# A seven-product matrix multiplication: block sums of the weights formed by accumulating loads instead of VectorE

## The chip, the cores and the metric

One Trainium2 chip, one of its cores. The metric is the device time of one launch, in microseconds (us); lower is better. The engines are TensorE (PE in the profile; its weight loads are PEld), VectorE (DVE), ScalarE (ACT), GpSimd (POOL) and SyncE (SP). SyncE and GpSimd issue the transfers from and to DRAM (DMA); a transfer's issue is an instruction in the issuing engine's queue, and the transfer itself runs on 16 DMA engines.

## The reference

A trunk of two layers on a sequence of 512 tokens with width 1024, in float32. Layer 0 mixes tokens by chunked attention, layer 1 by a chunked spatial gate; each is followed by a squared-ReLU net. All are preceded by a norm that is scaled and shifted by a conditioning vector.

```python
def chunked_spatial_gating(h, w_in, v_gain, w_s, b_s, w_out):
    z = jax.nn.gelu(h @ w_in, approximate=False)
    u, v = jnp.split(z, 2, axis=-1)
    v = rms_norm(v, v_gain).reshape(B, nw, SG_WINDOW, SG_GROUPS, SG_HALF // SG_GROUPS)
    ...
    return (u * vm.reshape(B, S, SG_HALF)) @ w_out

def squared_relu_mlp(h, w1, w2):
    return jnp.square(jax.nn.relu(h @ w1)) @ w2
...
for i in range(DEPTH):                       # DEPTH = 2
    mod = cond @ ada_w[i] + ada_b[i]
    sh1, sc1, g1, sh2, sc2, g2 = ...
    h = rms_norm(x, norm_mix[i]) * (1.0 + sc1) + sh1
    x = x + g1 * (attention(h) if i == 0 else spatial_gating(h))
    h = rms_norm(x, norm_ffn[i]) * (1.0 + sc2) + sh2
    x = x + g2 * squared_relu_mlp(h, ffn_w1[i], ffn_w2[i])
```

The net's hidden width is 4096, the gate's is 2 x 3072.

## The kernel before

**Precision.** Each float32 matrix is split into a high part (a cast to the matmul type float32r, by ScalarE) and a low part (the rest, by VectorE): class `Split`, lines 483 and 484, or lines 388 and 389 for plain weights. A product of two such matrices takes three matmuls (`mm3`, line 94), all of which are recorded at line 92. The operands live in 49 slots of 4 KB per partition of on-chip memory (`SL`), handed out in turn, so a load waits until the slot's last reader is through.

**Seven products.** Some weights are multiplied in a 2 x 2 block form with seven block products instead of eight (the Winograd form of Strassen's scheme): `seven`, line 616. The left matrix A (512 tokens by 1024) has blocks of 256 x 512, the weight B (1024 by 1024) has blocks of 512 x 512. With the blocks counted from 0, the products and the PSUM sums (z, y, v, w; each one bank per row tile) are

- 0: A00 B00 on z, 1: A01 B10 on y; C00 takes both
- 2: (A10 + A11)(B01 - B00) on v; C11 takes it
- 3: (A10 + A11 - A00)(B11 - B01 + B00) on z, behind product 0; C01 takes the sum
- 4: (A01 - A10 - A11 + A00) B11 on v, behind product 2; C01 takes the sum
- 5: (A00 - A10)(B11 - B01) on z; C10 and C11 take the sum
- 6: A11 (B10 - B11 + B01 - B00) on w; C10 takes it

`load` brings the four blocks of B, two transfers of 512 KB each, on SyncE's queue (line 625); `right` forms the differences on VectorE (line 631, 128 x 1024 elements an instruction) and splits them; `left.prep` forms the sums of A's blocks (line 530) and splits them; `mult` runs 24 matmuls of 512 columns (two row tiles `u`, four k, three terms) and then calls `put` for each row tile. `put` of class `Sum` copies the PSUM bank into the result on its first use (line 519, ScalarE) and adds it after that (line 517, VectorE). `put` of class `Gate` does the same (lines 1433 and 1435) and on the second use applies Gelu and a sum of squares (lines 1436 and 1438), and stores the tile to DRAM by GpSimd's queue (line 1410).

**Where it is used.** Eight weights: in each of the two nets, the first three quarters of the down projection (six weights, class `Spent` for the left side), and in the gate two of the three pairs of column blocks of v (two weights, class `Kept` for the left side, whose blocks are kept and reused). The remaining parts are plain products.

**Order.** `Run` (line 687) walks through a list of steps; a step's load is called `ll` steps ahead of its preparation and its preparation `lp` steps ahead of its product. In the nets (`ll` = `lp` = 3) a step of the up projection, also of 24 matmuls, is put between two of the seven products; in the third weight of each net the last two products have none between them. In the gate (`ll` = `lp` = 2) the 14 products of both weights follow one another. A planner with a model of the times orders each engine's queue, outside the stretches that fix TensorE's order by hand. Beside all this runs a queue of background work (`bg`, line 264) that loads and adds up the conditioning weights on VectorE (line 194); it is placed behind the last split (`mark`).

**Around the gate.** The first pair of v's column blocks is plain (`gate_tile`, line 442) and its second block's products stand directly ahead of the seven-product steps. Behind them `u_block` (line 1528) loads v back from DRAM.

## Time and profile before

| | us |
|---|---|
| median of three runs | 1412.46 (1410.62 to 1413.95) |
| the profiled execution | 1407.58, span 1405.8 |
| TensorE busy | 1383.6 (98%) |
| VectorE busy | 1021.7 (73%) |
| ScalarE busy | 711.3 (51%) |
| GpSimd busy | 15.7 (1%) |
| DMA engines, SyncE's queue | 45.9% of the span, 214.01 MB |

The profile is one execution. A group is a set of instructions of one line, engine and shape: its count, its busy time with the mean of one in ns, and the idle time of its engine ahead of them with what ended it ("released" it). The windows view gives busy times of the engines in a stretch of the span, the number of instructions behind each, TensorE's granted clock and the share of time that the DMA engines were busy. Idle time of an engine that isn't the bottleneck costs nothing.

### The profile page before, as it was taken

What the parts mean: (1) busy time and instruction counts of PE and PEld (TensorE: products, weight loads), DVE (VectorE), ACT (ScalarE), POOL (GpSimd) and SP (SyncE); (2) the same over time, 40 slices, a digit from 0 to 9 for tenths busy, and PEclk for the clock granted to TensorE, in tenths of its full rate; (3) what the DMA queues carried; (4) which work ended last, traced back from release to release, by engine and by line L of the source; (5) the groups of instructions that cost most, each with busy time, mean ns of one, the idle gap of its engine ahead of it and who ended that gap; (6) DMA issues with size and microseconds to landing.
All of it is one profiled execution on the core that took longest, in us unless ns stands there. A gap on an engine that the chain in (4) does not pass through costs nothing.

```text
span 1405.8 us, 18946 instructions
## 1 busy us (share of the span) xinstructions
PE 1383.6 (98%) x7226; PEld 1185.3 (84%) x7226; DVE 1021.7 (73%) x1494; ACT 711.3 (51%) x1229; POOL 15.7 (1%) x46
## 2 busy tenths in 40 slices
PE   9999998999999999999999999999999999999998
PEld 7899987789888888888888888888889988888887
DVE  7888998666667878777895746665677367766882
ACT  6547667555464544646586443223445455453630
POOL 0000000000000000000000000000000000000000
PEclk9999999999999999999999999999999999999999
DMA  9666566573253361456346535435437225242141
GB/s 374 242 172 206 162 174 195 179 270 106 75 195 119 123 222 60 138 192 240 135 157 236 184 100 176 151 127 165 142 113 270 76 90 180 71 140 90 31 165 60
DMA packets 85628, 221.53 MB, mean 158 GB/s; under 512 B 7960, under 2 KB 9376, under 8 KB 85536
## 3 DMA queue, kind: packets, MB, share of 16 engines
q1 hardware_dynamic: 83808, 214.01, 45.9%
q0 software_dynamic: 1728, 6.29, 1.1%
q8 instruction: 57, 0.93, 0.3%
q14 instruction: 35, 0.29, 0.1%
HBM read 197.21 MB, written 14.68 MB: 151 GB/s over the span
## 4 chain that ended last, share of the span: by engine, by line
PE 88%; DMA 5%; DVE 4%; ACT 2%; issue 1%; SPq 0%; DVEq 0%; ACTq 0%
PE p L92 86%; DMA s<-in_a_w_in 2%; DMA s<-in_ada_w 1%; PE p L1564 1%; DMA s<-in_a_w_out 1%; PE p L1238 1%; ACT s L483 1%; DVE s L1200 1%; PE p L315 1%; DVE s L1243 0%; DMA s<-in_b_w_in 0%; DVE s L955 0%; DMA s<-in_ffn_w 0%; DVE s L1267 0%; DVE s L1154 0%
## 5 line engine op out<-in xcount | busy, mean ns | idle before, releaser
L92 PE MATMUL p<-s,s 128*128 128x512 f32 (+2 forms) x6568 | 1322.6, 361 | 7.0 <-DVE nm L1200 2.0
L92 PEld LDWEIGHTS p<-s,s 128*128 128x128 f32 x6568 | 1109.5, 189 | 191.5 <-DVE nm L1200 3.0
L484 DVE TENSOR_TENSOR s<-s,s 128x1024 fp32r<-128x1024 f32 x234 | 280.0, 1220 | 115.5 <-ACT s L483 55.4
L483 ACT CAST s<-s 128x1024 fp32r<-128x1024 f32 x234 | 241.1, 1051 | 163.0 <-PE p L92 112.6
L389 DVE TENSOR_TENSOR s<-s,s 128x1024 fp32r<-128x1024 f32 x80 | 96.8, 1222 | 63.5 <-ACT s L388 51.1
L388 ACT CAST s<-s 128x1024 fp32r<-128x1024 f32 x80 | 83.5, 1051 | 92.6 <-DMA s<-in_b_w_in 36.2
L631 DVE TENSOR_TENSOR s<-s,s 128x1024 f32<-128x1024 f32 x64 | 77.6, 1220 | 32.0 <-DMA s<-in_ffn_w 31.6
L739 ACT ACTIVATE r<-p 128x512 f32<-128x512 f32 x64 | 38.1, 595 | 116.2 <-PE p L92 116.2
L194 DVE SCALAR_TENSOR_TENSOR s<-s,cs,s 128x1024 f32<-128x1024 f32 x70 | 89.6, 1280 | 5.7 <-DMA s<-in_ada_w 5.0
L517 DVE TENSOR_TENSOR s<-p,s 128x512 f32<-128x512 f32 x104 | 70.4, 685 | 19.1 <-PE p L92 17.9
L745 ACT ACTIVATE s<-r 128x256 f32<-128x256 f32 (+1 forms) x112 | 44.9, 443 | 1.2
L424 DVE TENSOR_TENSOR tr<-p,s 128x512 f32<-128x512 f32 (+1 forms) x33 | 22.0, 671 | 30.9 <-PE p L92 30.5
L1205 ACT ACTIVATE s<-s,nm 128x128 f32<-128x128 f32 (+3 forms) x64 | 36.0, 564 | 7.2 <-DVE nm L1200 5.6
L1200 DVE CUSTOM_DVE_ANT_0 s<-p,s 128x128 f32<-128x128 f32 (+3 forms) x64 | 29.7, 486 | 8.1 <-issue 4.7
L1569 ACT CAST s<-p 128x256 fp32r<-128x256 f32 x48 | 17.7, 370 | 34.9 <-PE p L1564 27.0
L530 DVE TENSOR_TENSOR s<-s,s 128x1024 f32<-128x1024 f32 x28 | 33.6, 1220 | 1.0 <-PE p L92 0.9
L1238 PE MATMUL p<-ident,s 128*128 128x128 f32 x160 | 25.0, 278 | 8.0 <-DVE s L1267 6.9
L304 ACT ACTIVATE s<-s 128x512 f32<-128x512 f32 x24 | 15.3, 638 | 33.9 <-DVE s L425 33.9
L1243 DVE TENSOR_TENSOR s<-p,s 128x512 fp32r<-128x512 f32 (+3 forms) x64 | 29.1, 485 | 3.7 <-ACT s L1242 3.3
L1570 DVE TENSOR_TENSOR s<-p,s 128x256 fp32r<-128x256 f32 x48 | 20.1, 418 | 15.4 <-ACT s L1569 15.4
L1242 ACT CAST s<-p 128x512 fp32r<-128x512 f32 (+3 forms) x64 | 24.9, 429 | 11.8 <-PE p L1238 11.4
L1543 DVE SCALAR_TENSOR_TENSOR s<-s,vr,gain 128x512 f32<-128x512 f32 x24 | 17.7, 748 | 16.8 <-PE p L92 11.7
(142 smaller groups left out, 755.5 us busy)
## 6 DMA issues: line engine op xcount, KB each, us to landing
s<-in_ffn_w SPq DMA_DIRECT2D x128, 512.0 KB, 4.6
s<-in_ada_w SPq DMA_DIRECT2D x96, 512.0 KB, 5.0
s<-in_b_w_in SPq DMA_DIRECT2D x48, 512.0 KB, 4.8
s<-in_b_w_out SPq DMA_DIRECT2D x24, 512.0 KB, 4.4
s<-in_a_w_in SPq DMA_DIRECT2D x22, 512.0 KB, 6.7
s<-s SPq DMA_DIRECT2D x64, 128.0 KB, 2.4
vd<-s POOLq DMA_DIRECT2D x12, 512.0 KB, 3.8
s<-vd SPq DMA_DIRECT2D x12, 512.0 KB, 3.6
```

Source lines behind the costliest of these rows:

```text
L92: T.matmul(ps, lhsT, rhs, start=start, stop=stop, skip_group_check=more)
L194: V.scalar_tensor_tensor(acc, r, ck, acc, ALU.mult, ALU.add)
L388: A.copy(hi, raw)
L389: engs[len(ids) // 2 % len(engs)].tensor_tensor(lo, raw, f32(hi), ALU.subtract)
L483: A.copy(self.hi, raw)
L484: mark[0] = V.tensor_tensor(self.lo, raw, f32(self.hi), ALU.subtract)
L517: V.tensor_tensor(dst, ps, dst, ALU.add)
L631: V.tensor_tensor(x[0], y_[0], z[0], ALU.subtract)
L739: A.activation(r, ps, AF.Relu)
L745: A.activation(d, v, AF.Square)
L1200: V.tensor_tensor_reduce(out=pt[it], in0=ps[:, 0:n], in1=b["bias"][:, 512 - n:512], scale=-1.0, scalar=-NEG, op0=ALU.add, op1=ALU.min, acc ...
L1238: T.transpose(ps[:, it * P:(it + 1) * P], b["pt"][it][:, jt * P:(jt + 1) * P], ident)
```

## The change

The scheme is rewritten with the signs of some blocks turned, so that every right operand is a running sum of blocks of B. Three tiles are loaded: x = B00, z = B10, y = B11. After a tile's split has been read, an accumulating transfer adds the next block of B from DRAM into the same tile: x becomes B00 + B01, then + B11, then + B10; y becomes B11 + B01. These transfers are issued on GpSimd's queue (`G.dma_start` with `accum_op`). The minus signs go to the left sums and to `put`, which now takes the operation (add or subtract). The products run in the order 0, 1, 2, 4, 3, 5, 6 on the sums z, y, v, v, z, z, z: product 6 goes onto the open sum z, and C10 takes that sum alone. In the gate C10 is read by Gelu from PSUM (`whole`). The left sum for product 3 is formed together with that for product 4.

```diff
-        def put(self, t, hf, ps):
+        def put(self, t, hf, ps, op=ALU.add, whole=True):
 ...
-                V.tensor_tensor(dst, ps, dst, ALU.add)
+                V.tensor_tensor(dst, dst, ps, op)
...
@@ class Spent, prep (class Kept alike)
-                self.comb("x", (1, 0), (1, 1), ALU.add)
-            elif m == 3:
+                self.comb("x", (1, 0), (1, 1), ALU.subtract)
+            elif m == 4:
                 self.comb("x", "x", (0, 0), ALU.subtract)
-            elif m == 4:
-                self.comb((0, 1), (0, 1), "x", ALU.subtract)
+                self.comb((0, 1), (0, 1), "x", ALU.add)
...
@@ seven
-        def load(i, j):
-            raw[i, j] = []
+        def block(i, j, s_):
+            r0 = i * 512 + s_ * 256
+            return src[r0:r0 + 256, j * 512:j * 512 + 512].rearrange("(k p) n -> p k n", p=P)
+
+        def load(name, i, j):
+            raw[name] = []
             for s_ in range(2):
                 t, n = SL.get([P, 2, 512], F32)
-                r0 = i * 512 + s_ * 256
-                SP.dma_start(t, src[r0:r0 + 256, j * 512:j * 512 + 512].rearrange("(k p) n -> p k n", p=P))
-                raw[i, j].append((t, n))
-
-        def sub(d, a, b):
-
-            for x, y_, z in zip(raw[d], raw[a], raw[b]):
-                V.tensor_tensor(x[0], y_[0], z[0], ALU.subtract)
...
-        def right(m):
-            if m == 2:
-                sub((0, 0), (0, 1), (0, 0))
-            elif m == 3:
-                sub((0, 0), (1, 1), (0, 0))
-            elif m == 5:
-                sub((0, 1), (1, 1), (0, 1))
-            elif m == 6:
-                sub((1, 0), (1, 0), (0, 0))
...
+                SP.dma_start(t, block(i, j, s_))
+                raw[name].append((t, n))
+
+        def right(m, name, add):
+
+            op[m] = []
+            for s_, (t, n) in enumerate(raw[name]):
+                op[m].append(Split(t, [P, 2, 512]))
+                if add is None:
+                    SL.free(n)
+                else:
+                    G.dma_start(t, block(*add, s_), accum_op=ALU.add)
...
         plan = (
-            (True, ((0, 0),), False),
-            (True, ((0, 0),), True),
-            (True, ((1, 1),), False),
-            (False, ((0, 1),), False),
-            (False, ((0, 1),), True),
-            (False, ((1, 0), (1, 1)), True),
-            (True, ((1, 0),), True),
+            (0, ("x", 0, 0), ("x", (0, 1)), ("z", True, ((0, 0, add, False),), False)),
+            (1, ("z", 1, 0), ("z", None), ("y", True, ((0, 0, add, False),), True)),
+            (2, None, ("x", (1, 1)), ("v", True, ((1, 1, add, False),), False)),
+            (4, ("y", 1, 1), ("y", (0, 1)), ("v", False, ((0, 1, add, False),), True)),
+            (3, None, ("x", (1, 0)), ("z", False, ((0, 1, sub, False),), False)),
+            (5, None, ("y", None), ("z", False, ((1, 1, sub, False),), False)),
+            (6, None, ("x", None), ("z", False, ((1, 0, add, True),), True)),
         )
...
@@ class Gate, put
-            if (t, hf) not in self.seen:
+            if not whole and (t, hf) not in self.seen:
                 self.seen.add((t, hf))
                 A.copy(dst, ps)
                 return
-            V.tensor_tensor(dst, ps, dst, ALU.add)
-            A.activation(dst, dst, AF.Gelu)
+            if not whole:
+                V.tensor_tensor(dst, dst, ps, op)
+            A.activation(dst, ps if whole else dst, AF.Gelu)
```

More of the change, by code (lines that the diff above doesn't have):

```diff
@@ L573, in prep @@
                 return
[L574 to L577 removed]
+            for c in {
+                2: (("x", (1, 0), (1, 1), ALU.subtract),),
+                4: (("x", "x", (0, 0), ALU.subtract), ((0, 1), (0, 1), "x", ALU.add)),
+                5: (((0, 0), (0, 0), (1, 0), ALU.subtract),),
+            }.get(m, ()):
+                self.comb(*c)
             self.op[m] = Split(self.ab[("x", "x", (0, 1), (0, 0))[m - 2]][0], [P, 4, 256])
[L579 removed]
+            self.spend(*((), ("x",), ((0, 1),), ((0, 0), (1, 0), (1, 1)))[m - 2])
         def comb(self, d, a, b, o):
@@ L654, in mult @@
                 p, pi = ps[acc, u]
+                start = first
                 c = slice(u * P, u * P + P)
@@ L657, in mult @@
                     bh, bl = b[k // 2].hi[:, k % 2, :], b[k // 2].lo[:, k % 2, :]
-                    mm3(p, a.hi[:, k, c], a.lo[:, k, c], bh, bl, first and k == 0, k == 3, not first)
-                for i, j in outs:
-                    y.put(2 * i + u, j, p)
+                    mm3(p, a.hi[:, k, c], a.lo[:, k, c], bh, bl, start and k == 0, k == 3, not start)
+                for i, j, o, whole in outs:
+                    y.put(2 * i + u, j, p, o, whole)
                 if done:
@@ L665, in mult @@
                 x.free()
+        add, sub = ALU.add, ALU.subtract
         plan = (
-            (True, ((0, 0),), False),
-            (True, ((0, 0),), True),
-            (True, ((1, 1),), False),
-            (False, ((0, 1),), False),
-            (False, ((0, 1),), True),
-            (False, ((1, 0), (1, 1)), True),
-            (True, ((1, 0),), True),
+            (0, ("x", 0, 0), ("x", (0, 1)), ("z", True, ((0, 0, add, False),), False)),
[5 more added lines that the diff above has]
+            (6, None, ("x", None), ("z", False, ((1, 0, add, True),), True)),
         )
-        blocks = ((0, 0), (1, 0), (0, 1), (1, 1))
         return [
             Step(
-                (lambda m=m: load(*blocks[m])) if m < 4 else nothing,
-                lambda m=m: right(m),
+                (lambda b=b: load(*b)) if b else nothing,
+                lambda m=m, r=r: right(m, *r),
                 lambda m=m: left.prep(m),
-                lambda m=m: mult(m, *plan[m]),
+                lambda m=m, p=p: mult(m, *p),
             )
-            for m in range(7)
+            for m, b, r, p in plan
         ]
@@ L1424, in __init__, with put @@
             self.p, self.seen = p, set()
-        def put(self, t, hf, ps):
+        def put(self, t, hf, ps, op, whole):
             cb = 2 * self.p + hf
```

20 lines of the change are left out of this document (3 added, 17 removed).

## The prediction

> **What bounds the kernel now.** I read the page first, then the 25 us windows, then what TensorE waited for.
>
> ```profile
> span 1405.8 us, 18946 instructions
> ...
> PE 1383.6 (98%) x7226; PEld 1185.3 (84%) x7226; DVE 1021.7 (73%) x1494; ACT 711.3 (51%) x1229; POOL 15.7 (1%) x46
> ...
> q1 hardware_dynamic: 83808, 214.01, 45.9%
> q0 software_dynamic: 1728, 6.29, 1.1%
> ...
> L631 DVE TENSOR_TENSOR s<-s,s 128x1024 f32<-128x1024 f32 x64 | 77.6, 1220 | 32.0 <-DMA s<-in_ffn_w 31.6
> ...
> L517 DVE TENSOR_TENSOR s<-p,s 128x512 f32<-128x512 f32 x104 | 70.4, 685 | 19.1 <-PE p L92 17.9
> ```
>
> TensorE is busy for 1383.6 of 1405.8 us, so 22.2 us is all that any edit beside it could return. The question is where these 22.2 us lie.
>
> ```profile
> core 0: us, PE busy (x) PEld busy (x) DVE busy (x) ACT busy (x) POOL busy (x), PEclk, DMA share, GB/s
> ...
> 225.00:250.00 25.00, 20.74 (x124) 18.55 (x123) 16.97 (x37) 15.47 (x37) 0.90 (x3) 0.93 0.65 206
> 250.00:275.00 25.00, 21.59 (x113) 18.14 (x112) 17.39 (x34) 16.26 (x32) 0.61 (x1) 0.93 0.51 172
> ...
> 500.00:525.00 25.00, 25.00 (x112) 20.69 (x111) 19.25 (x20) 9.41 (x15) 0.00 (x0) 1.00 0.68 236
> ...
> 700.00:725.00 25.00, 24.95 (x110) 20.36 (x109) 24.48 (x25) 19.40 (x31) 1.06 (x2) 1.00 0.40 126
> ...
> 1025.00:1050.00 25.00, 24.67 (x114) 20.11 (x113) 18.14 (x34) 7.99 (x22) 0.00 (x0) 1.00 0.23 85
> ```
>
> Each row is one window: its length, then busy time and instruction count for each engine, the granted clock, the DMA share. The windows with real holes lie before 300 us, in the first projections and the attention, which the diff doesn't touch. The first block difference of the seven-product steps starts at 343.1 us:
>
> ```profile
> L631 DVE TENSOR_TENSOR s<-s,s x64: 1212/1218/1228, 343.1 to 1302.4; 128x1024 f32<-128x1024 f32 x64
> ```
>
> From 300 us on only two windows up to 1400 us are under 25.00: 0.05 us at 700 and 0.33 us at 1025. A busy TensorE could still be a slow one, so I look at counts: a window full of 512-column products holds 112 of them (0.223 us each), and the window at 700 us holds 110. It lost two, some 0.45 us. That is the whole prize inside the code that is changed.
>
> ```profile
> PEld p L92 <- DVE s L389: 0.8, 1, 0.8
> PEld p L92 <- ACT s L1433: 0.5, 1, 0.5
> ```
>
> This is the list of TensorE's waits after 300 us: two of note. The one of 0.5 us is the gate's, released by a copy out of PSUM; it agrees with the two products lost. The other is released by a plain weight's split and belongs to the window at 1025 us.
>
> **The change, part by part.** A product is 24 matmuls before and after (two row tiles, four k, three terms), and a weight of seven blocks has seven. So TensorE's own term is 0 us.
>
> *Taken off VectorE.* Eight weights with four block differences of two halves each are the 64 instructions of line 631: 77.6 us. The last product now lands on the open sum that held the other terms, so one of eight `put`s per row tile goes: 12 of line 517 in the six feed-forward weights (12 x 0.685 = 8.2 us). In the gate's two weights four copies and four adds go, by line 517's price 2.7 us on VectorE. Sum 88.5 us of VectorE, 66% of the span instead of 73%. On the path that sets the end this is worth only what TensorE lost to it: at most the 0.45 us at 700 us. I take -0.4; bounds -0.45 and 0.
>
> *Added loads.* 64 plain loads on SP's queue become 48, and 64 accumulating ones of 512 KB are issued on GpSimd's. The trace has no accumulating load. The nearest rows are the plain loads and GpSimd's own stores:
>
> ```profile
> L1410 POOL DMA_DIRECT2D vd<-s x12: 531/531/673, 657.0 to 768.4; - x12
> ...
> DMA to landing us min/median/max: 2.9/3.8/8.0
> ```
> ```profile
> s<-in_b_w_in SPq DMA_DIRECT2D x48, 512.0 KB, 4.8
> ```
>
> Issue costs GpSimd about 0.53 us; it is 1% busy, so 64 x 0.53 = 34 us there is covered. Landing: 3.8 us from below (GpSimd's store, median; nothing to add). From above I take two such transfers one after the other, 4.8 + 4.8 = 9.6 us, since the old contents have to be read as well. I work with 7 us, nearer to the double because the bytes read do double.
>
> Is 7 us hidden? In the feed-forward nets an up-projection step stands between two down-projection steps, 24 matmuls each. The running sum is read by the split at places 0, 2, 4 and 6 of the new order (products 0, 1, 2, 4, 3, 5, 6), so between two readings lie four steps of 24 x 0.223 = 5.4 us: 21 us. Into these go two casts and two subtractions of the split (L483 at 1051 ns, L484 at 1220 ns) and the landing:
>
> ```profile
> L484 DVE TENSOR_TENSOR s<-s,s 128x1024 fp32r<-128x1024 f32 x234 | 280.0, 1220 | 115.5 <-ACT s L483 55.4
> L483 ACT CAST s<-s 128x1024 fp32r<-128x1024 f32 x234 | 241.1, 1051 | 163.0 <-PE p L92 112.6
> ```
>
> 2 x 1.05 + 2 x 1.22 + 7 = 11.5 us (14.1 at the upper bound): covered twice over or nearly. In the gate no other steps lie between, so the distance is two steps, 10.7 us, against 11.5: each of three links slips by 0.8 us (3.4 at the upper bound), 2.4 us in all (10.2), against a lead of two steps, 10.7 us. Covered, without cover left at the upper bound. SP's queue gains: 16 issues less, and no block waits for a slot of its own. On GpSimd's queue the gate's stores of `vd` can stand behind a waiting accumulation; their loads back belong to the stage behind the gate, and who waits before that is a split that needs the store's slot. On ScalarE a cast that waits for an accumulation holds the PSUM copies queued behind it. I put 0 us on all of this, with the price of a miss among the rivals.
>
> *DMA share.* One 512 KB load occupies the engines for 45.9% x 1405.8 / 214.01 MB x 0.524 MB = 1.58 us.
>
> ```profile
> 350.00:600.00 250.00, 250.00 (x1116) 207.22 (x1115) 191.22 (x191) 127.79 (x174) 0.00 (x0) 1.00 0.41 135
> 600.00:690.00 90.00, 90.00 (x415) 74.86 (x414) 68.40 (x79) 46.90 (x94) 1.74 (x3) 1.00 0.53 189
> 690.00:767.00 77.00, 76.95 (x343) 63.38 (x342) 61.86 (x63) 58.04 (x97) 4.86 (x10) 1.00 0.53 178
> ```
>
> The first feed-forward net (three weights, 24 accumulations more and 6 loads less in 250 us) goes from 0.41 to 0.52 at one load's price, and to 0.41 + (24 x 3.16 - 6 x 1.58) / 250 = 0.68 at the double. The gate (77 us, 16 more and 4 less) goes from 0.53 to 0.78, or at the double to 0.53 + (16 x 3.16 - 4 x 1.58) / 77 = 1.10. But its 16 loads don't all lie there:
>
> ```profile
> L625 SPq DMA_DIRECT2D s<-in_b_w_in x16: 368/378/419, 615.2 to 715.7; - x16
> ```
> ```profile
> 690.23 25.88 SPq L625 DMA_DIRECT2D s<-in_b_w_in  x8
> ```
>
> Eight are issued before 690 us, from 615.2 us on. Spread over 600 to 767 us (167 us at 0.53) the double gives 0.79. So 0 us here too.
>
> The Trainium skill, page "Collectives: The Full Stack", section "The bandwidth ceiling: the fold count and why AG ≠ RS ≠ AR", says that an add inside the DMA engine runs at half the rate of a copy, as it emits two source reads on one ring. By that rule the double is the price, and the gate's 1.10 would be a rival (below); no row here shows an accumulation.
>
> *Order on PSUM.* This is the term that I see against the change. The old order alternates banks: z, y, v, z, v, z, w. The new one is z, y, v, v, z, z, z. A bank that has just been read out by `put` is written again by the next product, and that product's first row tile must wait until `put` is through. In the feed-forward nets a step lies between, 2.7 + 5.4 us of grace. In the gate (six reuses a weight, two weights), and where the last two products of each net's third weight stand together (two a net), the grace is one row tile: 12 x 0.223 = 2.7 us. 16 reuses in all. How late do these read-outs finish today? In this timeline the gate's 336 matmuls end where line 1505 starts; counting back 0.227 us each, as the run of 294 in 67.18 us gives, dates the end of each row tile.
>
> ```profile
> 699.31 67.18 PE L92 MATMUL p<-s,s 128*128 128x512 f32 x294
> ...
> 706.63 0.57 ACT L1433 COPY s<-p 128x512 f32<-128x512 f32 x1
> ...
> 710.75 0.57 ACT L1433 COPY s<-p 128x512 f32<-128x512 f32 x1
> ...
> 722.82 1.28 DVE L1435 TENSOR_TENSOR s<-p,s 128x512 f32<-128x512 f32 x2
> ...
> 752.82 0.58 ACT L1433 COPY s<-p 128x512 f32<-128x512 f32 x1
> ...
> 766.33 1.03 PE L1505 MATMUL p<-ident,s 128*128 128x128 f32 x8
> ```
>
> The third product's tiles ended at 703.7 and 706.4; their copies finished at 707.2 and 711.3, 3.5 and 4.9 us later: 0.8 and 2.2 us beyond the grace. The fifth product's second tile ended at 717.3 and was added by 723.5, 3.5 us beyond. In the second weight the tile of 750.0 was copied by 753.4, 0.7 us beyond. With today's lateness the new order would therefore stall TensorE, for up to some 8 us (0.8 + 2.2 + 3.5 in the first weight, about 1.5 for the rest of both). But the lateness of the first weight comes from VectorE, which the row of 700 us shows at 24.48 of 25.00, and the change takes 16 x 1.22 + 2.7 = 22 us from it around the gate. Bounds 0 and 8; I take 1.6, a fifth, since the cause goes and the planner that orders the queues sees the reuse.
>
> *Left blocks.* Four sums of left blocks before and after. One moves from the place of product 3 to that of product 4, one step earlier, with its 1.22 us; no DMA goes with it. Nothing.
>
> **Sum.** 0 - 0.4 + 0 + 1.6 = +1.2 us on the profiled execution, 1407.6 (span 1405.8 and 1.8 around it), so 1408.8 there. The median shown is 1412.46, 4.9 us above the profiled execution, for no cause that the trace shows; I carry it along: 1412.5 + 1.2 = 1413.7. This is no change: about 0.2%, 2.8 us, is what a measurement of this kernel can tell.
>
> **Rivals.**
> 1. *The next product waits for the read-out of its own bank* (slower). Place: the gate, steps three to seven of each weight. It decides once read-outs end more than 2.7 us after their tile. For it: the lateness above, and casts in ScalarE's queue that now wait for accumulations ahead of the copies. Against: 22 us less on VectorE. At two thirds of the upper bound, 5.5 - 0.4 = +5: 1417.5.
> 2. *The accumulations cost double and fill the gate's DMA* (slower). At a share of 1.10 the 77 us stretch by 10%, +7.7: 1420. For it: doubled reads. Against: half of the gate's loads were issued before 690 us, which gives 0.79. The half rate of the Trainium skill's page named above has this outcome.
> 3. *Accumulations far dearer than twice a load* (slower). At four loads' engine time (6.3 us) the first net's share is 0.41 + (24 x 6.3 - 9.5) / 250 = 0.98, and the links no longer fit into 21 us beside other loads. For six weights at, say, 5 us late each, and the gate: +35, 1447. Nothing in the trace speaks for it but that the operation is absent.
> 4. *Faster.* Waits beside the two in the list would have to be in the changed part; the counts show none. What could do it is the 20 us of holes before 300 us or the 4.9 us between the profile and the median, if they move with another plan. At -4: 1408.5.
>
> **Chances.** Hidden, as summed: 0.52, its own range 1411 to 1416. Rival 1: 0.20. Rival 2: 0.10. Rival 3: 0.07. Rival 4: 0.11. The range goes from 1409 to 1421: it leaves out rival 3, half of rival 4 and the far ends of 1 and 2. Slower by over 0.2%: rivals 2 and 3, 0.17 of rival 1, and 0.04 of the hidden case, 0.38. Faster: 0.11 and 0.01, 0.12. Same: 0.50.
>
> **What would show it.** Right: line 631's group is gone, `put` on VectorE falls from 104 to 92, GpSimd's queue has 64 more DMAs, windows from 350 us on stay at 25.00 with 112 products, VectorE near 933 us. The landing of GpSimd's loads (7 us forecast; 3.8 to 9.6) and the DMA share of 350 to 600 us (0.52 to 0.68) test the middle part. Rival 1 shows as TensorE's waits on line 519 or the gate's copy and add between 690 and 770 us; rivals 2 and 3 as casts of line 483 waiting for the weights' DMA, followed by idle TensorE. The forecast is wrong if TensorE loses or gains more than 3 us after 300 us.

## The result, and the profile after

The changed kernel takes 1434.98 us (1430.98 to 1438.53, four runs) against 1411.54 us for the kernel before in the same comparison (1407.74 to 1413.95, four runs): a ratio of 1.0167, interval 1.0141 to 1.0193. It is slower by 23 us. The forecast was 1413.7 us with a range up to 1421, so the time lies outside it.

The page of the changed kernel: span, busy times, the two queues (packets, MB, share of 16 engines' span), then three groups and issues (issues end with the median us from issue to landing).

```profile
span 1431.5 us, 19079 instructions
...
PE 1392.5 (97%) x7226; PEld 1190.9 (83%) x7226; DVE 942.9 (66%) x1414; ACT 710.6 (50%) x1225; POOL 93.3 (7%) x110
...
q1 hardware_dynamic: 79456, 205.63, 43.2%
q0 software_dynamic: 19136, 39.85, 15.3%
...
L637 POOL DMA_DIRECT2D s<-in_ffn_w x48 | 58.0, 1210 | 791.6 <-DVE ru L137 310.4
...
L519 DVE TENSOR_TENSOR s<-s,p 128x512 f32<-128x512 f32 x92 | 62.6, 684 | 46.7 <-PE p L92 46.5
...
s<-in_ffn_w POOLq DMA_DIRECT2D x48, 512.0 KB, 6.0
s<-in_b_w_in POOLq DMA_DIRECT2D x16, 512.0 KB, 7.2
```

VectorE got its relief (1021.7 to 942.9 us, 80 instructions fewer), and it was worth nothing. TensorE runs the same 7226 instructions, but it is idle for 39.0 us of its span (22.2 before) and busy for 8.9 us longer. These 16.8 and 8.9 us are the 25.7 us by which the spans differ. The windows say where:

```profile
350.00:600.00 250.00, 250.00 (x1121) 207.44 (x1120) 167.62 (x167) 128.07 (x174) 26.52 (x22) 1.00 0.65 168
...
690.00:830.00 140.00, 123.19 (x537) 100.63 (x536) 71.33 (x95) 73.88 (x123) 18.95 (x22) 0.94 0.70 190
...
700.00:725.00 25.00, 20.52 (x84) 16.46 (x83) 13.44 (x13) 13.11 (x21) 4.16 (x4) 0.93 0.82 194
725.00:750.00 25.00, 24.62 (x109) 20.07 (x108) 8.88 (x9) 14.49 (x24) 6.88 (x7) 1.00 0.73 161
750.00:775.00 25.00, 17.42 (x68) 13.36 (x67) 13.16 (x13) 13.22 (x22) 3.31 (x6) 0.86 0.80 216
...
800.00:825.00 25.00, 20.62 (x98) 17.47 (x97) 15.97 (x29) 9.51 (x19) 0.00 (x0) 0.86 0.55 186
```

The feed-forward net (350 to 600 us) is full, with more matmuls than before in the same 250 us (1121 against 1116). The gate and the first block behind it are not. The same 140 us of the kernel before:

```profile
690.00:830.00 140.00, 139.95 (x656) 116.40 (x655) 105.31 (x134) 87.02 (x146) 5.39 (x11) 1.00 0.53 180
```

656 matmuls against 537: 119 missing, 26.5 us at 0.223 us each. This window's count is a yardstick for the experiments below. It is a rough one, since the matmuls in it aren't all of one size. What TensorE waited for in the changed kernel (us in total, times, longest), in the whole run:

```profile
PE p L92 <- ACT s L1424: 10.9, 2, 6.4
...
PE p L1556 <- DVE s L1551: 4.4, 1, 4.4
...
PE p L92 <- DVE s L1427: 1.5, 2, 1.1
```

The first row is two waits for a copy of the gate out of PSUM. The other engines' waits between 690 and 780 us tell why that copy was late:

```profile
ACT s L485 <- DMA s<-in_b_w_in: 31.3, 12, 4.8
...
DVE s L486 <- ACT s L485: 37.9, 11, 7.2
```

ScalarE stood still for 31.3 us in casts that waited for a load, and VectorE behind it. In the same stretch of the kernel before (there the split's cast is line 483) it was 2.3 us:

```profile
ACT s L483 <- DMA s<-in_b_w_in: 2.3, 1, 2.3
```

The timeline of the first wait (start, length, engine, line; in brackets the idle time before and what ended it):

```profile
699.73 10.13 PE L92 MATMUL p<-s,s 128*128 128x512 f32 x44
...
703.63 1.20 POOL L637 DMA_DIRECT2D s<-in_b_w_in  x1 [6.21 <-DVE s L486]
...
711.48 1.04 ACT L485 CAST s<-s 128x1024 fp32r<-128x1024 f32 x1 [4.15 <-DMA s<-in_b_w_in]
712.43 0.62 ACT L1428 ACTIVATE s<-s 128x512 f32<-128x512 f32 x1
...
713.72 0.56 ACT L1424 COPY s<-p 128x512 f32<-128x512 f32 x1
...
714.34 3.88 PE L92 MATMUL p<-s,s 128*128 128x512 f32 x9 [4.48 <-ACT s L1424]
...
762.38 3.99 PE L92 MATMUL p<-s,s 128*128 128x512 f32 x9 [6.45 <-ACT s L1424]
```

An accumulation is issued at 703.63 and has landed at 711.48, 7.85 us later. ScalarE's next instruction in its queue is the cast that needs it, for a product that is still to come. Behind that cast stands the copy of product 2's first row tile, which TensorE finished about 707.2 us (one row tile, 12 matmuls, ahead of the end at 709.86). Product 4 goes onto the same bank and can't start before the copy is done: 4.48 us of idle TensorE. The last row is the second long wait, with the same releaser, at the same place of the second weight.

The last two rows of TensorE show a second cost: the first nine matmuls behind the waits take 3.88 and 3.99 us, 0.43 us each and more instead of 0.223. That is some 1.9 us for each wait, and the granted clocks of 0.93 and 0.86 in the windows agree with it. Behind the third long wait, that for line 1551, it is the same:

```profile
809.70 4.19 PE L92 MATMUL p<-s,s 128*128 128x512 f32 x9
```

These three account for some 6 of the 8.9 us that TensorE is busy for longer. Another 1.0 us lies before 300 us (282.96 us busy against 281.94), which the edit doesn't touch; where the rest lies isn't shown.

### The profile page after: what moved, and what is told of

It is laid out like the page before. It is cut to its first block, busy times and chain, and to the rows that moved or that the text cites. A ratio compares the mean times of both kernels' runs of the same rounds, so it can differ in the third digit from the quotient of the medians.

```text
span 1431.5 us, 19079 instructions
## 1 busy us (share of the span) xinstructions
PE 1392.5 (97%) x7226; PEld 1190.9 (83%) x7226; DVE 942.9 (66%) x1414; ACT 710.6 (50%) x1225; POOL 93.3 (7%) x110
## 3 DMA queue, kind: packets, MB, share of 16 engines
q0 software_dynamic: 19136, 39.85, 15.3%
## 4 chain that ended last, share of the span: by engine, by line
PE 80%; DMA 7%; issue 5%; DVE 4%; ACT 2%; POOL 1%; SPq 0%; DVEq 0%; POOLq 0%; ACTq 0%
PE p L92 77%; DMA s<-in_a_w_in 1%; DMA s<-in_b_w_in 1%; DMA s<-in_ada_w 1%; DMA s<-in_ffn_w 1%; DMA vd<-s 1%; PE p L1556 1%; PE p L1229 1%; DVE s L946 1%; POOL s L637 1%; DMA s<-in_a_w_out 1%; PE p L315 1%; DMA s<-in_x 0%; DMA s<-in_b_w_out 0%; DVE s L389 0%
## 5 line engine op out<-in xcount | busy, mean ns | idle before, releaser
L92 PE MATMUL p<-s,s 128*128 128x512 f32 (+2 forms) x6568 | 1330.4, 363 | 19.4 <-ACT s L1424 10.9
L637 POOL DMA_DIRECT2D s<-in_ffn_w x48 | 58.0, 1210 | 791.6 <-DVE ru L137 310.4
L519 DVE TENSOR_TENSOR s<-s,p 128x512 f32<-128x512 f32 x92 | 62.6, 684 | 46.7 <-PE p L92 46.5
L532 DVE TENSOR_TENSOR s<-s,s 128x1024 f32<-128x1024 f32 x28 | 33.6, 1221 | 3.4 <-PE p L92 3.1
L1537 ACT CAST s<-s 128x512 fp32r<-128x512 f32 x24 | 14.7, 622 | 31.9 <-PE p L92 15.6
```

Source lines behind the costliest of these rows:

```text
L92: T.matmul(ps, lhsT, rhs, start=start, stop=stop, skip_group_check=more)
L519: V.tensor_tensor(dst, dst, ps, op)
L637: G.dma_start(t, block(*add, s_), accum_op=ALU.add)
```

## The experiments

Each kernel was compared with the kernel before on the same chip; all ratios are to it.

### Which part loses

*Accumulations in the nets alone.* The gate keeps the old `seven`.

```diff
-        steps += seven(kept, ..., Gate(p))
+        steps += seven_old(kept, ..., Gate(p))     # the code before
```

> Only the six weights of the two nets use the accumulating loads; the gate's two weights go the old way (differences on VectorE, old order, old banks). Theory A (the whole loss is made in the gate, where no other step lies between two products): the time is that of the kernel before, 1411.5 us, within 3 us, and TensorE's busy time from 350 to 600 us stays at 250. Theory B (accumulating loads cost wherever they are, by their doubled engine time): six of the eight weights keep three quarters of the loss, 1425 to 1431.

Measured: 1411.03 us, ratio 1.0006 (0.9996 to 1.0016). In the six net weights the accumulations are hidden and worth nothing.

*Accumulations in the gate alone.* The reverse, for the nets' six weights.

```diff
-    steps = seven(Spent...)
+    steps = seven_old(Spent...)
```

> The other half: only the gate's two weights use the accumulating loads, the nets go the old way. Theory A: 1432 to 1437, the loss of the changed kernel. Theory B: a quarter of the loss, 1415 to 1420.

Measured: 1431.53 us, ratio 1.0154 (1.0139 to 1.0170). The loss is the gate's.

*The new order without the accumulations.* Signs, order of products and banks are the new ones; the four blocks come as plain loads into tiles of their own on SyncE's queue, and VectorE adds them up.

```diff
-                    G.dma_start(t, block(*add, s_), accum_op=ALU.add)
+            if add is not None:
+                for (t, _), (b, _) in zip(raw[name], raw[add]):
+                    V.tensor_tensor(t, t, b, ALU.add)
```

> New signs, new order of the products, new banks (z, y, v, v, z, z, z), last product on the open sum, but all blocks come by plain loads on SyncE's queue into tiles of their own and VectorE adds them up. Theory A1 (the copies out of PSUM are late because ScalarE waits for accumulating loads ahead of them): no stall, 1409 to 1415. Theory R1 (the new order by itself: a bank is written again one row tile, 2.7 us, after its last use): at least half of the loss stays, 1423 or more.

Measured: 1409.64 us, ratio 1.0000 (0.9988 to 1.0012). Its window:

```profile
690.00:830.00 140.00, 139.93 (x656) 116.36 (x655) 106.78 (x134) 86.23 (x142) 5.40 (x11) 1.00 0.55 180
```

656 matmuls, none lost. Reusing a bank right behind its read-out costs nothing by itself.

### The accumulations: waited for, or too many bytes?

*Plain loads in the accumulations' place.* GpSimd's loads overwrite the tile instead of adding to it; the sums of the right blocks are left out. The splits still wait for them.

```diff
-                    G.dma_start(t, block(*add, s_), accum_op=ALU.add)
+                    G.dma_start(t, block(*add, s_))
```

> The changed kernel, but the 64 loads on GpSimd's queue don't accumulate: each overwrites the tile at the same place, behind the same split (so the sums of blocks are left out and the output isn't the reference's). Same dependence, same queue, half the engine time. Theory A2 (the landing of an accumulating load, twice a plain load's engine time, is what the gate can't hide): landing falls from about 7 to about 5 us in the gate, the time to 1411 to 1419. Theory R5 (the dependence on the split and GpSimd's 1.2 us issue are enough, whatever the load does): 1426 or more.

Measured: 1417.99 us, ratio 1.0062 (1.0045 to 1.0080). Window and TensorE's waits between 690 and 830 us:

```profile
690.00:830.00 140.00, 134.23 (x617) 111.60 (x616) 80.70 (x107) 81.25 (x135) 14.22 (x23) 0.99 0.63 210
```
```profile
PE p L1556 <- DVE s L1551: 4.1, 1, 4.1
PE p L92 <- DVE s L1427: 1.7, 1, 1.7
```

39 matmuls are lost instead of 119, and the waits for the gate's copies are gone. What stays is 1.7 us of waiting for an addition in the gate and one wait in the first block behind it.

*The same on SyncE's queue.*

```diff
-                    G.dma_start(t, block(*add, s_))
+                    SP.dma_start(t, block(*add, s_))
```

> As the run above, but these plain loads are issued on SyncE's queue among the others (the sums are left out again). It takes GpSimd's issue time away and puts the waiting loads ahead of other loads in SyncE's queue. Theory A2: as the run above, within 4 us of it. If GpSimd's issue is what costs, this is faster than the run above by 5 us or more; if the loads held up behind a waiting one in SyncE's queue matter, it is slower by as much.

Measured: 1421.33 us, ratio 1.0089 (1.0069 to 1.0108). With plain loads, GpSimd's queue is not the obstacle.

*Half the bytes.* In the gate each accumulation brings one of the tile's two row groups; half of each sum of the gate's right blocks is left out.

```diff
-                    G.dma_start(t, block(*add, s_), accum_op=ALU.add)
+                    G.dma_start(t[:, 0:o, :], block(*add, s_)[:, 0:o, :], accum_op=ALU.add)   # o = 1 in the gate
```

> The changed kernel, but in the gate each accumulating load brings only the first half of its rows (the other half of each block sum is left out). Engine time and a part of the landing halve, the dependence stays. Theory A2: landing near 5 us, the time falls by half of the loss or more, to 1412 to 1423. Theory R5: 1430 or more.

Measured: 1424.32 us, ratio 1.0100 (1.0084 to 1.0116), 580 matmuls in the window. So the loss grows with how long an accumulation takes: 8.7 us with plain loads, 14 with half, 23 with whole ones. That fits a wait as well as a shortage of DMA time.

*Accumulations that nobody reads.* They go into two spare tiles. The splits read the loaded tiles as they are, so the sums of the gate's right blocks are left out.

```diff
-                    G.dma_start(t, block(*add, s_), accum_op=ALU.add)
...
+                    G.dma_start(dead[s_][0], block(*add, s_), accum_op=ALU.add)
```

> The changed kernel, but the gate's sixteen accumulating loads go into two tiles of their own that nobody reads: the same transfers from DRAM with the same issue on GpSimd's queue and the same double reading, while the splits read the three loaded tiles as they are. The sums of the gate's right blocks are left out. Theory A (the loss comes from splits that wait for the accumulations, and from what stands behind these splits): the waits in the gate go, 1409 to 1419 us, the upper end if the wait in the first block behind the gate stays. Theory B (bytes on the DMA engines, or GpSimd's work, whoever waits): 1426 us or more.

Measured: 1428.54 us, ratio 1.0123 (1.0103 to 1.0143), a number for theory B. But nothing held the accumulations back any longer, and they ran packed together. The window ahead of the loss, and TensorE's one long wait:

```profile
675.00:700.00 25.00, 25.00 (x112) 20.71 (x111) 12.45 (x11) 10.13 (x19) 7.79 (x7) 1.00 1.02 213
```
```profile
PE p L92 <- ACT s L232: 15.0, 1, 15.0
```

At a DMA share of 1.02, as this view counts it, TensorE still runs its full 112 matmuls. The 15 us are a wait behind a late load of the conditioning weights (line 232 splits what they add up to). So this run decides nothing: the accumulations have to stand at their old times.

*The same, each accumulation tied to its split.* A one-element copy on GpSimd reads the split's low part, and the accumulation is issued behind it; v's stores go to ScalarE's queue, so that they don't stand behind the spare tiles' accumulations.

```diff
+                        r = G.tensor_copy(read, f32(op[m][-1].lo[:, 0, 0:1]))
+                        with tc.issue_after(r.ins):
+                            G.dma_start(dead[s_][0], block(*add, s_), accum_op=ALU.add)
```

> The changed kernel with v's stores on ScalarE's queue (1437.6 us by itself), and the gate's sixteen accumulating loads go into two tiles that nobody reads; each is issued behind a one-element read of its split by GpSimd, so the transfers come about when they come in the changed kernel. The splits read the loaded tiles as they are. The sums of the gate's right blocks are left out. Theory A (the loss comes from splits that wait for the accumulations, and from the read-outs behind them): no waits of TensorE on read-outs between 690 and 780 us, 1410 to 1421 us. Theory B (the bytes, the issues on GpSimd, or the accumulations' slowing of other transfers): 1428 us or more.

Measured: 1417.3 us, ratio 1.0051 (1.0026 to 1.0077).

*Its control*: the changed kernel with only v's stores on ScalarE's queue.

```diff
-        G.dma_start(vd[cb, b], v.rearrange("p t n -> p (t n)"))
+        A.dma_start(vd[cb, b], v.rearrange("p t n -> p (t n)"))
```

> The changed kernel with one edit: the gate's twelve stores of v are issued on ScalarE's queue instead of GpSimd's, so no store stands behind an accumulation that waits and no accumulation behind a store that waits. Nothing is left out. Theory A (the chain, and casts ahead of read-outs): the same loss, 1430 to 1438 us. Theory E (stores and accumulations hold each other up in GpSimd's queue): 1412 to 1426.

Measured: 1437.62 us, ratio 1.0175 (1.0150 to 1.0201). The stores' queue isn't the cause. First the control's windows, then those of the kernel with unread accumulations:

```profile
690.00:780.00 90.00, 74.41 (x307) 59.41 (x306) 41.06 (x41) 48.43 (x76) 14.01 (x14) 0.94 0.79 187
```
```profile
690.00:780.00 90.00, 87.20 (x376) 70.27 (x375) 50.98 (x52) 57.70 (x92) 20.42 (x26) 0.98 0.90 223
```

The issues of the gate's accumulations lie in about the same stretch, first in the control, then with the accumulations unread:

```profile
L637 POOL DMA_DIRECT2D s<-in_b_w_in x16: 1203/1203/1304, 661.2 to 756.3; - x16
```
```profile
L642 POOL DMA_DIRECT2D s<-in_b_w_in x16: 1198/1203/2398, 668.6 to 756.5; - x16
```

TensorE's longest waits between 690 and 830 us, in the same order:

```profile
PE p L92 <- ACT s L1424: 13.0, 4, 7.7
```
```profile
PE p L92 <- ACT s L485: 0.9, 1, 0.9
...
PE p L92 <- DVE s L1432: 0.8, 1, 0.8
```

The waits for the gate's copies are gone; one wait of 0.8 us for a read-out (line 1432) is left. This is the answer. The same sixteen accumulating transfers, in about the same stretch and at a higher DMA share (0.90 against 0.79), cost 17 us less (1.0175 to 1.0051) when no split waits for them. Bytes and issues are not what TensorE loses most of its time to; the splits that wait are. Whether the bytes have a part in the 0.5% that is left isn't shown.

### What the waiting does to the queues

*Product 4 on a bank of its own*, so that it needn't wait for product 2's copy; C01 is then made of three read-outs.

```diff
-            (4, ..., ("v", False, ((0, 1, add, False),), True)),
+            (4, ..., ("w", True, ((0, 1, add, None),), True)),
```

> The changed kernel, but product 4 gets a bank of its own instead of following product 2 on v; C01 is put together from three read-outs, so product 4 never waits for the copy of product 2. Theory A1: the two long waits of TensorE for line 1424 (4.5 and 6.4 us) go, and what follows from them: 1415 to 1424. Theory R4 (the operands themselves come too late, the bank only shows it first): TensorE waits the same time for a split instead, 1431 or more.

Measured: 1429.43 us, ratio 1.0139 (1.0124 to 1.0154). TensorE's waits there:

```profile
PE p L92 <- DVE s L1427: 8.3, 2, 6.6
PE p L1499 <- POOL s L1496: 6.1, 1, 6.1
```

The first wait isn't gone, it has moved to VectorE's read-out on z, which stands behind a subtraction that waits for a cast that waits for an accumulation. The second row is another matter: there GpSimd's memset of line 1496 waits for the load of the spatial weights (`in_b_w_s`), which this edit doesn't touch.

*Read-outs first.* In the gate the splits of the product two steps on are issued behind the present product's read-outs, on ScalarE and VectorE.

```diff
+                    for r in list(readout.values()):
+                        es.enter_context(tc.issue_after(r.ins))
                     getattr(self.steps[j], part)()        # part "right" or "left"
```

> The changed kernel, but in the gate the splits of two steps ahead stand behind the PSUM read-outs of the present product in ScalarE's and VectorE's queues. Theory A1 (read-outs wait in an in-order queue behind splits that wait for accumulating loads): most of the loss goes, 1412 to 1421. Theory R4 (the operands come too late however the queues are ordered): TensorE waits for splits instead, 1428 or more.

Measured: 1432.57 us, ratio 1.0165 (1.0148 to 1.0182). Now TensorE waits for the splits themselves:

```profile
PE p L92 <- ACT s L485: 9.8, 2, 6.1
PE p L92 <- ACT s L388: 3.2, 1, 3.2
```

No order of these two queues that was tried serves both: with the casts ahead the read-outs are late, with the read-outs ahead the splits are. Behind the read-outs a split has, by the code, only about one step left (5.4 us), so this edit also takes lead away.

*A third step of lead* in the gate.

```diff
-    run = Run(steps, 2, 2)
+    run = Run(steps, 2, 3)
```

> One edit on the changed kernel: in the gate the preparations run three steps ahead of their products instead of two. Nothing is left out. Theory A (each running sum's chain of split, issue and landing is about as long as the two steps, 10.7 us, between its readings, and casts that wait for it stand in ScalarE's queue ahead of the read-outs): a third step of lead gives 5.4 us that the slips can use up, but the distance between two readings stays at two steps and the casts stay ahead of the read-outs, so the stalls get smaller and don't go: 1417 to 1428 us. Theory B (the accumulations' bytes fill the DMA engines or hold TensorE back at any spacing): 1430 to 1437, no change against the changed kernel.

Measured: 1433.87 us, ratio 1.0171 (1.0153 to 1.0188). This went against the expectation: the edit is worth nothing. By the code it moves the first reading ahead and leaves the distance between two readings of a tile as it is. But the trace shows that it hardly moved anything. The issues of the gate's accumulations in the changed kernel, then with the third step, and a wait that the third step's kernel still has:

```profile
L637 POOL DMA_DIRECT2D s<-in_b_w_in x16: 1177/1201/1308, 659.0 to 751.9; - x16
```
```profile
L637 POOL DMA_DIRECT2D s<-in_b_w_in x16: 1177/1196/1678, 660.0 to 753.9; - x16
```
```profile
PE p L92 <- ACT s L1424: 9.9, 2, 8.6
```

So the run doesn't show what a real third step of lead is worth.

### More distance between the readings

*TensorE's order written out* through the gate, a control.

```diff
-    any_order()
     run = Run(steps, 2, 2)
...
     run.go()
+    any_order()
```

> One edit on the changed kernel: TensorE's order through the gate's seven-product steps is written out, product by product, instead of left to the planner, which starts single matmuls of a product early and mixes two products. It is the control for the two kernels below. Nothing is left out. Theory A: TensorE's order isn't the cause, its waits for the read-outs of products 2 (on v) stay: 1428 to 1440 us. A rival C (the planner's mixing of the products on TensorE makes the stalls): 1412 to 1420.

Measured: 1437.78 us, ratio 1.0200 (1.0178 to 1.0222). The planner's order on TensorE isn't the cause of the loss.

*Plain tiles between the steps.* On top of it, the four plain tiles of the first pair's second block are put between the seven-product steps.

```diff
-    for t in range(NT):
-        gate_tile(1, t, ws[1][0])
-    run.go()
+    for i in range(len(steps)):
+        if i % 7 in (2, 4):
+            gate_tile(1, i // 7 * 2 + (i % 7 == 4), ws[1][0])
+        run.tick()
```

> The control with one more edit: the four tiles of the first pair's second column block (24 matmuls each, plain) are not multiplied ahead of the seven-product steps but between them, one behind product 1 and one behind product 4 of each weight. The same transfers, the same splits, the same TensorE work; only the distance between two readings of a running sum grows there from two steps (10.7 us) to three (16.1 us). Nothing is left out. Theory A: the chain fits, the two waits of 4 to 6 us in the gate go, and what is left is the wait at the gate's end and the first block behind it (about 4 us and the clock behind it): 1413 to 1420 us. Theory B (bytes at any spacing): 1428 or more.

Measured: 1435.62 us, ratio 1.0183 (1.0165 to 1.0202): a miss, no clear gain on the control, and a number for theory B. VectorE's waits between 655 and 800 us name a new obstacle:

```profile
DVE s L486 <- DMA vd<-s: 22.4, 3, 11.7
DVE s L486 <- ACT s L485: 20.8, 11, 5.4
```

For 22.4 us splits waited for a slot that a store of v still held. These stores share GpSimd's queue with the accumulations.

*The same with v's stores on ScalarE's queue*, by the edit shown above for the control of the unread accumulations.

> The kernel with the plain tiles between the seven-product steps and TensorE's order written out (1435.6 us), with one more edit: the stores of v on ScalarE's queue. Nothing is left out. If the wider spacing didn't help because splits waited for slots whose stores stood behind accumulations (22 us of VectorE's waits on the stores): these waits fall under 8 us, and 1418 to 1428 us, 6 us of it for TensorE's wait of 6 us at 658 us that the written order brings along. If the slots come late for another reason: 1432 to 1438.

Measured: 1427.42 us, ratio 1.0109 (1.0089 to 1.0129). By the ratios this is 10 us better than with the stores on GpSimd's queue, and 13 us better than the control. The waits for stores fell from 22.4 to 15.4 us, not below 8 as expected. TensorE's waits between 655 and 830 us:

```profile
PE p L92 <- ACT s L485: 6.0, 1, 6.0
PE p L92 <- ACT s L1424: 5.2, 2, 4.4
```

The 6.0 us are those that the written order brings along at 658 us; the control has the same row. *One plain tile ahead*, in the place that the planner gave it, should take them out:

```diff
+    gate_tile(1, 0, ws[1][0])
     for t in range(2, NT):
         gate_tile(0, t, ws[0][0])
...
-        if i % 7 in (2, 4):
+        if i in (2, 9, 11):
```

> The kernel with plain tiles between the seven-product steps, TensorE's order written out and v's stores on ScalarE's queue (1427.4 us), with one edit: the first tile of the second column block is multiplied ahead of the last two tiles of the first, as the planner did, so that TensorE doesn't wait 6 us at 658 us; three plain tiles are left to stand between the steps (behind product 1 of the first weight, products 1 and 4 of the second). Nothing is left out. Theory A: those 6 us and the clock behind them go, what is left is a wait or two of 4 us in the gate: 1414 to 1422 us. Theory B: 1425 us or more.

Measured: 1427.03 us, ratio 1.0123 (1.0099 to 1.0147), a miss. The 6.0 us are gone, but with one plain tile fewer between the steps the waits for copies are back at

```profile
PE p L92 <- ACT s L1424: 10.2, 2, 6.9
```

Distance between the readings helps, in part; the accumulations could not be hidden in the gate this way.

### The end of the gate

*Hold back one split.* The weight of the first output projection is split behind the first two multiplications of line 1551, in the changed kernel.

```diff
+                with tc.issue_after(first_u[0, 1].ins) if blocks == [0] else nullcontext():
                     w, ids = wload(src[:, hf * 512:hf * 512 + 512], len(act))
```

> The changed kernel with one edit: the weight of the first output projection (in_b_w_out, plain loads and splits) is split behind the first two multiplications of line 1551 in the first block behind the gate, so that its subtraction doesn't stand ahead of them on VectorE. Nothing is left out. If the wait of 4.4 us on line 1551 and the lower clock behind it come from that subtraction (and its cast) waiting for a late load: 1427 to 1432 us. If the wait only moves on: 1433 to 1437.

Measured: 1430.08 us, ratio 1.0133 (1.0112 to 1.0153), against 1.0167 without: 4.8 us by the ratios, though the intervals overlap. The wait on line 1551 is gone from the list. In the changed kernel it looked like this:

```profile
806.05 1.04 ACT L388 CAST s<-s 128x1024 fp32r<-128x1024 f32 x1 [4.28 <-DMA s<-in_b_w_out]
...
807.13 1.22 DVE L389 TENSOR_TENSOR s<-s,s 128x1024 fp32r<-128x1024 f32 x1 [4.08 <-ACT s L388]
808.27 1.65 DVE L1551 SCALAR_TENSOR_TENSOR s<-p,bsT,s 128x384 f32<-128x384 f32 x4
...
808.93 1.11 PE L1556 MATMUL p<-ident,s 128*128 128x128 f32 x4 [4.38 <-DVE s L1551]
```

It is the same pattern with a plain load: a cast waits for the load of this weight, VectorE's subtraction waits for the cast, and the multiplication of line 1551 that TensorE needs stands behind both.

*The same edit on the kernel with spread tiles* (v's stores on GpSimd's queue).

> The kernel with the plain tiles between the steps and one more edit: the weight of the first output projection (in_b_w_out, plain loads and splits) is loaded and split behind the first two multiplications of line 1551 in the first block behind the gate, so that its cast and subtraction can't stand ahead of them on ScalarE and VectorE. Nothing is left out. Theory A with the same mechanism at the gate's end (a cast of a late load queued ahead of work that TensorE needs): TensorE's wait on line 1551 of some 4 us goes too: 1409 to 1414 us, within 3 us of the kernel before. Rival D (the end's loss has another cause, such as v's late stores or the late last product): no gain over the kernel with the tiles spread, within 1.5 us of it.

Measured: 1435.9 us, ratio 1.0186 (1.0165 to 1.0208), no gain. The written order had already moved line 1551's wait away, so there was nothing to hold.

Every kernel is planned anew, so an edit shifts more than itself; what is read above are differences of some 5 us and more, with the wait that goes or comes beside them. No run took the read-outs out of the queues in which the casts wait. That the gate's loss comes from splits that wait for accumulations is thus shown by an experiment; that the wait reaches TensorE through these two queues is read from the timelines. Two things stay open: why some 7 us remain where nothing waits for accumulations (1.0051 and 1.0062; in the first of them ScalarE's casts of line 388 wait 16.2 us for plain loads between 655 and 830 us), and whether an order of the queues exists that hides accumulations in the gate.

## Why the prediction was wrong

**TensorE's own work, left blocks: right.** 7226 instructions before and after; the new order alone is 1.0000.

**Taken off VectorE: right in kind.** Line 631 is gone, `put` went from 104 to 92, and 80 instructions fewer were counted, as forecast. 88.5 us were forecast and 78.8 measured, which leaves 942.9 us where 933 were named. In the two traces the durations of VectorE's instructions add up to 87.5 us less (1104.2 to 1016.8), as forecast; the page's busy time counts overlapping instructions once and fell by less. It was worth nothing, as said.

**Price of an accumulation: right.** Landing 6.0 us (nets) and 7.2 us (gate) against 7, which was a choice between bounds of 3.8 and 9.6. Engine time: GpSimd's queue kept the engines for 15.3% of 1431.5 us, 219 us; the stores of v are 1.1% x 1405.8 = 15 us of it. The other 204 us over 64 accumulations are 3.18 us each, 2.0 times the plain load's 1.58 us. The Trainium skill, page "Collectives: The Full Stack", section "The bandwidth ceiling: the fold count and why AG ≠ RS ≠ AR", has the adding step of a collective at half the rate of the copying one, because it reads two sources, and limits its model to rings of three ranks or more. The ratio in this trace agrees; whether the accumulating load here is slower for that reason no run shows. GpSimd's issue was mis-sized, 1.20 us instead of 0.53, without effect.

**The nets: right.** 21 us between two readings cover the chain; a DMA share of 0.65 from 350 to 600 us (0.52 to 0.68 forecast), every 25 us of that stretch full, and the nets alone at 1.0006.

**The gate: here it failed.** The step is "each of three links slips by 0.8 us (3.4 at the upper bound), 2.4 us in all (10.2), against a lead of two steps, 10.7 us. Covered, without cover left at the upper bound". The sizes in it were about right: 7.85 us from issue to reading in the timeline, and with two casts and two subtractions 7.85 + 2 x 1.05 + 2 x 1.22 = 12.4 us, where 11.5 were taken. The conclusion was not. A lead protects the product that the split is for. It doesn't protect what stands behind the split in its engine's queue, and that was the read-outs, which have one row tile, 2.7 us. The prediction saw it ("On ScalarE a cast that waits for an accumulation holds the PSUM copies queued behind it") and put 0 us on it. That 0 is the term that failed. Measured, ScalarE waits 31.3 us in these casts, and TensorE 10.9 us in two waits for copies behind them. The lead did cover the splits: among TensorE's waits in the changed kernel there is none for lines 485 and 486. Unread accumulations, 17 us faster, show that the waiting is the cause. The third step of lead says nothing on this, since its accumulations were issued no earlier.

**Order on PSUM: a size of 1.6 us by itself, 0 measured.** The bank reuse costs nothing as long as read-outs are on time: 1.0000, and that with a VectorE as busy as before (106.78 us in the window against 105.31), so the relief that was to remove the cause wasn't needed. It is the place where late read-outs are charged, not the cause; with another bank for product 4 the charge only moved to z.

**Rival 1 was the right mechanism with too small a price.** It named the place, the gate's banks, and the casts in ScalarE's queue. Its 5 us came from the lateness of the old read-outs and from VectorE's load, not from the new waits. Measured are 16.8 us more idle time on TensorE, and 8.9 us more busy time, for which there was no term at all: some 6 us of it is the clock behind the three long waits. The trace of before had it in view (0.93 in the two windows with holes at 225 and 250 us). The Trainium skill, page "TensorE: Matmul & The Clock Gate", section "Why this matters for your kernels", warns of idle gaps over some 3 us, behind which the clock is halved; nine matmuls in 3.88 us behind a gap of 4.48 us agree.

**Rival 2 was wrong as a mechanism.** The share in the gate rose to 0.86 (690 to 767 us), but with unread accumulations, at 0.90, TensorE is idle for 2.8 of 90 us instead of 15.6 in the control at 0.79, and in the one window at 1.02 it is full. That it has a part in the 7 us or so that stay open isn't ruled out. The signs that the prediction named didn't separate it from rival 1: casts that wait for the weights' loads, and TensorE's waits for the gate's copies, both came. It took the unread accumulations to tell them apart. **Rival 3** did not occur: an accumulation costs twice a load, not four times. **Rival 4** did not occur.

**The gate's end was not foreseen.** The forecast looked at loads that the change moves. The load of the next weight, whose code it doesn't touch, came late: 4.4 us of waiting on line 1551 and some 2 us of clock behind it. Holding that weight's split back returned 4.8 us, with intervals that overlap.

## What to carry to other kernels

Work taken off an engine that isn't the bound was worth nothing here, and a transfer that takes its place puts its landing into a chain. Compare that chain with the time between two readings of the same tile: 21 us hid it here, 10.7 us didn't, though the lead looked long enough. For each instruction that will wait, write down what stands behind it in its engine's queue and how much grace that has; here it was 2.7 us. Price each TensorE wait of over 4 us with another 2 us for the clock behind it, as in the three waits of 4.38 to 6.45 us here.

## What the runs showed of the hardware

An accumulating load of 512 KB from DRAM kept the DMA engines for 3.18 us, twice a plain load's 1.58 us. Its issue kept GpSimd for 1.20 us; a plain load of the same shape issued there took 0.72 us, a store of v mostly 0.53 to 0.60 us. A DMA share of 1.02 over 25 us did not slow TensorE, whose 112 matmuls took the whole window and no more. Behind waits of 4.48 and 6.45 us TensorE ran nine matmuls in 3.88 and 3.99 us, about half speed, before it was back at full speed.
